# Small reciprocal roots as one GpSimd power, and a broadcast read with step zero

## The chip, the cores and the metric

The kernel runs on one core of one Trainium2 chip. Its time is the device time of one execution in microseconds (us); lower is better. The engines named below are TensorE (PE, with its weight loads shown as PEld), VectorE (DVE), ScalarE (ACT), GpSimd (POOL) and SyncE (SP), which work side by side and wait for one another through semaphores.

## The reference

The program is a small two-layer encoder over 512 positions of width 1024, all in 32-bit floats. Layer 0 mixes with an RWKV-7 recurrence (12 heads of 64) beside a 4-head attention into 256 memory tokens; layer 1 uses chunked attention beside the same kind of memory attention. Each layer ends with a convolutional gated feed-forward block. What matters here are its reciprocal roots:

```
def rms_norm(x, g):
    xf = x.astype(jnp.float32)
    y = xf * lax.rsqrt(jnp.mean(xf * xf, axis=-1, keepdims=True) + RMS_EPS)
    return (y * g.astype(jnp.float32)).astype(x.dtype)
...
kk = kk / jnp.maximum(jnp.sqrt(jnp.sum(kk * kk, axis=-1, keepdims=True)), 1e-12)
...
y = (y - mean) * lax.rsqrt(var + LN_X_EPS) * per_head(lnx_w) + per_head(lnx_b)
```

The first is a norm over the width of each position, and there are seven uses of it in the kernel (the input, the memory, one before each feed-forward block, one between the layers, and the last one in two halves). The other two are per head and position: the length of the key, and the variance of the recurrence's output.

## The kernel before, in words

Activations lie transposed: 128 features on the partitions, the 512 positions along the free axis, eight such tiles for the width. A weight tile of 128 x 1024 is loaded (`load_w`), split into a rounded part and a remainder (`split_w`, L169 to L175), and `dense` multiplies with three matmuls per 128 x 128 block: L198 and L199 with the rounded weight, L203 with its remainder. While `lo_on` is set, in the middle of layer 0, the remainder isn't made by a DVE subtraction (L175) but by an ACT pass (L172) and an accumulating DMA that the GpSimd queue issues (L173).

Layer 0's mixer goes over six pairs of heads. `prepare(i)` projects key, receptance and value of a pair, normalises the key, and solves a triangular system per chunk with a long row of small DVE instructions (L662 to L669: `X`, tile Xs, with the product in Xu). `front(i)` builds the matrices of the pair's eight chunks, and `back(i)` runs the recurrence over them and normalises its output. `weave` interleaves three such generators: back of pair i-1, front of pair i, prepare of pair i+1. A generator yields a cost and a wait in ns; `weave` gives the turn to the one that is furthest behind its share, and a yielded wait holds that generator back by so much on weave's own clock. The stream that results isn't the final order: a planner of the language places each instruction on its engine by priority (the order of the stream) and by when it reckons the operands ready, with its own durations for each instruction. So an instruction that it takes to be late lets later ones pass, on each engine apart.

The roots are used in two helpers.

`head_rsqrt` (L541) is used once in `prepare` through `keys` (L626, the key's length) and once in `back` (L850, the output's variance), so twelve times in all. The squares of a 128 x 512 tile are summed by four small matmuls per call into eight columns (L550), a DVE instruction adds or clamps (`fix`, tile hra), `rsqrt_small` makes the roots, the generator yields 700 with a wait of 3000, a DVE copy spreads each column over 64 columns (L556), and four PE transposes (L559) turn the result so that it can be multiplied with the tile.

`norm_rho` (L242) is used seven times. Four matmuls against a column of 1/1024 (L245, two in the last norm's halves and in the memory's), a DVE addition of the epsilon (L247, tile rha), `rsqrt_small` on four or two columns, a DVE copy that spreads each column over 128 (L252), PE transposes (L255) and an ACT copy into `rho` (L256), which scales the projections as they leave PSUM.

`rsqrt_small` (L219) works on 128 x n values with n of 8, 4 or 2: one DVE instruction makes a first guess from the bits of the number (L222), and three Newton rounds of three DVE instructions each (L224, L225, L226) follow, so ten dependent instructions on DVE.

Of the kernel before, what the change touches and what calls it, by code (L numbers as in the profile page):

```python
# [111 lines left out]
def trunk_kernel(ctx, tc, A, out):  # L112
# [17 lines left out]
    acc = cp.tile([P, S], F32, name="acc")  # L130
    rho = cp.tile([P, S], F32, name="rho")
    rc = cp.tile([P, 4], F32, name="rc")

    def C(name, lo=0, n=None):
        o, w = COFF[name]
        return cst[:, o + lo:o + lo + (w if n is None else n)]
# [23 lines left out]
    def tmp(dt=F32, shape=(P, S)):  # L160
        return banks["tmp"].tile(list(shape), dt, name="tmp", tag="tmp")
# [54 lines left out]
        V.tensor_tensor(l_, src, h_, op=ALU.subtract)  # L216


    def rsqrt_small(pool, a, n):  # L219
        r = pool.tile([P, 8], F32, name="rsq", tag="rsq")  # L220
        q = pool.tile([P, 8], F32, name="rsq2", tag="rsq2")
        V.tensor_scalar(r[:, :n].bitcast(I32), a.bitcast(I32), -0.5, 1597463007.0, op0=ALU.mult, op1=ALU.add)  # L222
        for _ in range(3):
            V.tensor_tensor(q[:, :n], r[:, :n], r[:, :n], op=ALU.mult)  # L224
            V.scalar_tensor_tensor(q[:, :n], q[:, :n], -0.5, a, op0=ALU.mult, op1=ALU.mult)  # L225
            V.scalar_tensor_tensor(r[:, :n], q[:, :n], 1.5, r[:, :n], op0=ALU.add, op1=ALU.mult)  # L226
        return r


    def norm_tile(src, m, gain, h_, l_):  # L230
        sq = acc if m == 0 else tmp()
# [10 lines left out]
    def norm_rho(acc_, rho_, n=4, rc_=None):  # L242
        ps = ps_s()
        for t in range(n):
            PE.matmul(ps[:, 2 * t:2 * t + 2], acc_[:, t * P:(t + 1) * P], C("ones_d"), start=True, stop=True)  # L245
        a = cp.tile([P, 8], F32, name="rha", tag="rha")
        V.tensor_scalar(a[:, :n], ps[:, 0:2 * n:2], RMS_EPS, None, op0=ALU.add)  # L247
        r = rsqrt_small(cp, a[:, :n], n)
        if rc_ is not None:
            V.tensor_copy(rc_[:, :n], r[:, :n])  # L250
        bc = tmp()
        V.tensor_copy(bc[:, :n * P].rearrange("p (t c) -> p t c", c=P), r[:, :n].unsqueeze(2).to_broadcast([P, n, P]))  # L252
        pt = ps_s()
        for t in range(n):
            PE.transpose(pt[:, t * P:(t + 1) * P], bc[:, t * P:(t + 1) * P], C("ident"))  # L255
        SC.copy(rho_, pt[:, :n * P])  # L256

    def mem_attention(l, score, cost, dst, pr_tile, pt_tile):
# [139 lines left out]
    def kt_(name, shape=(P, S), bufs=None, dt=F32):  # L398
        if bufs is None:
            return kp.tile(list(shape), dt, name=name, tag=name)  # L400
        return kp.tile(list(shape), dt, name=name, tag=name, bufs=bufs)
# [141 lines left out]

    I64 = COFF["i64"][0]

    def head_rsqrt(sq, sel, fix, bank):

        ps = bank()
        for t in range(4):
            PE.matmul(ps[:, 2 * t:2 * t + 2], sq[:, t * P:(t + 1) * P], C(sel), start=True, stop=True)  # L550
        a = kt_("hra", (P, 8), bufs=2)
        fix(a[:], ps[:, 0:8])
        r = rsqrt_small(kp, a[:], 8)
        yield 700, 3000
        bc = tmp()
        V.tensor_copy(bc[:].rearrange("p (g c) -> p g c", c=64), r[:].unsqueeze(2).to_broadcast([P, 8, 64]))  # L556
        pt = bank()
        for t in range(4):
            PE.transpose(pt[:, t * P:(t + 1) * P], bc[:, t * P:(t + 1) * P], C("ident"))  # L559
        yield pt  # L560
# [5 lines left out]
    def prepare(i, T):  # L566
# [54 lines left out]
        def keys():  # L621
# [1 line left out]
            SC.activation(kn[:], k[:], AF.Copy, scale=kneg[:, i:i + 1])  # L623
            sq = tmp()
            SC.activation(sq[:], kn[:], AF.Square)
            hr = head_rsqrt(sq, "hs1", lambda o, p: V.tensor_scalar(o, p, 1e-24, None, op0=ALU.max), ps_s)  # L626
            yield next(hr)
            pr_ = next(hr)
            V.tensor_tensor(kn[:], kn[:], pr_[:], op=ALU.mult)
# [138 lines left out]
    def back(i, T, dst, tiles=own_tiles, go=None):  # L768
# [78 lines left out]
        sq = tmp()  # L847
        SC.activation(sq[:], yc[:], AF.Square)
        yield 0, 1700
        hr = head_rsqrt(sq, "hsm", lambda o, p: V.tensor_scalar(o, p, LN_X_EPS, None, op0=ALU.add), ps_s)  # L850
        yield next(hr)
        pr_ = next(hr)
        if go is not None:
# [427 lines left out]
```

## Time and profile before

| what | value |
|---|---|
| median of three runs | 1376.41 us (1375.87 to 1377.62) |
| profiled execution, span from the first to the last instruction | 1375.2 us |
| PE busy | 1320.1 us, 96% of the span |
| DVE busy | 827.1 us, 60% |
| ACT busy | 612.6 us, 45% |
| POOL busy | 34.0 us, 2%, in 55 instructions |
| mean granted TensorE clock | 0.989 |

The profile is of an execution of its own, so its span stands beside the median of the timed runs, 1.2 us below it; a time of that execution other than its span isn't on the page. A busy share is an average over stages: from about 55 us to 390 us layer 0's mixer runs, with many small instructions on PE and DVE; the two feed-forward blocks (about 410 to 775 us and 1000 to 1365 us) are rows of large matmuls; layer 1's attention lies between them. In the rows, a line such as `L224 DVE TENSOR_TENSOR rsq<-rsq` is an instruction of line 224 on DVE that writes and reads the tile rsq; in the chain of waits each row has its start, its length and the instruction that the end of the program goes back to.

### The profile page before, as it was taken

How to read it: one execution, taken by the hardware profiler on the slowest of the kernel's cores; microseconds unless marked ns; L12 is line 12 of the kernel's file. 1: busy time of each engine (PE TensorE's matmuls, PEld its weight loads, DVE VectorE, ACT ScalarE, POOL GpSimd, SP SyncE). 2: the span in 40 equal slices, each digit the busy share in tenths (PEclk: the TensorE clock that was granted, in tenths of full speed). 3: DMA queues.
4: the chain of work that ended last, by engine and by line, in shares of the span. 5: the costliest groups of instructions: out<-in, count | busy, mean ns of one | idle time of the engine just before them, and what ended most of it. 6: DMA issues, size and time to landing. Idle time of an engine off the chain costs nothing.

```text
span 1375.2 us, 20877 instructions
## 1 busy us (share of the span) xinstructions
PE 1320.1 (96%) x8266; PEld 1073.8 (78%) x8266; DVE 827.1 (60%) x1752; ACT 612.6 (45%) x1022; POOL 34.0 (2%) x55
## 2 busy tenths in 40 slices
PE   6989999999799999999999999999999999999996
PEld 4877777777588888888888878786788888888886
DVE  7876788878356655655333667657665565563324
ACT  6556565555234333333222566657443333332321
POOL 3000000000000000000000000000000000000000
PEclk9999999999899999999999999999999999999998
DMA  5366544462132233233232422222223223223332
GB/s 181 112 181 135 107 104 111 104 135 50 52 117 92 92 100 100 92 97 99 84 98 85 157 87 85 82 94 94 92 92 107 92 93 103 96 88 86 106 91 75
DMA packets 63507, 139.18 MB, mean 101 GB/s; under 512 B 24625, under 2 KB 28337, under 8 KB 63409
## 3 DMA queue, kind: packets, MB, share of 16 engines
q1 hardware_dynamic: 60672, 127.89, 29.8%
q0 software_dynamic: 2736, 9.96, 4.2%
q8 instruction: 65, 1.06, 0.3%
q14 instruction: 34, 0.27, 0.1%
HBM read 131.01 MB, written 6.82 MB: 100 GB/s over the span
## 4 chain that ended last, share of the span: by engine, by line
PE 78%; DVE 12%; ACT 4%; DMA 3%; issue 2%; SPq 0%; DVEq 0%; ACTq 0%; POOLq 0%
PE psf L198 12%; PE psf L199 12%; PE psf L203 12%; PE psd L198 10%; PE psd L199 10%; PE psd L203 10%; DVE Xu L667 2%; DVE Xs L669 1%; PE pss L1098 1%; DVE Xs L662 1%; DVE ML L720 1%; DVE wlo L175 1%; PE psd L1048 1%; PE pss L297 1%; ACT whi L169 1%
## 5 line engine op out<-in xcount | busy, mean ns | idle before, releaser
L175 DVE TENSOR_TENSOR wlo<-wraw,whi 128x1024 fp32r<-128x1024 f32 x183 | 219.0, 1197 | 132.3 <-PE psd L203 118.2
L169 ACT CAST whi<-wraw 128x1024 fp32r<-128x1024 f32 (+1 forms) x202 | 207.8, 1030 | 163.9 <-DMA wraw<-in_ffn_out_dram 41.5
L198 PE MATMUL psd<-r1h,whi 128*128 128x512 f32 x336 | 137.6, 410 | 7.5 <-ACT r1h L215 3.8
L198 PE MATMUL psf<-r2h,whi 128*128 128x512 f32 x352 | 137.1, 390 | 0.0
L198 PE MATMUL psf<-r1h,whi 128*128 128x512 f32 x352 | 137.1, 390 | 0.0
L199 PE MATMUL psf<-r1l,whi 128*128 128x512 f32 x352 | 136.9, 389 | 0.0
L199 PE MATMUL psf<-r2l,whi 128*128 128x512 f32 x352 | 136.9, 389 | 0.0
L199 PE MATMUL psd<-r1l,whi 128*128 128x512 f32 x336 | 134.9, 401 | 0.2 <-DVE r1l L216 0.2
L203 PE MATMUL psd<-r1h,wlo 128*128 128x512 f32 x336 | 91.3, 403 | 3.9 <-DMA wlo<-in_wA_dram 3.9
L199 PE MATMUL psd<-f3l,whi 128*128 128x512 f32 (+1 forms) x238 | 88.6, 377 | 0.0
L198 PE MATMUL psd<-f3h,whi 128*128 128x512 f32 (+1 forms) x238 | 88.5, 376 | 0.0
L359 DVE TENSOR_TENSOR tmp<-psf,rho 128x512 f32<-128x512 f32 x44 | 30.4, 692 | 94.7 <-PE psf L203 94.7
L203 PE MATMUL psf<-r1h,wlo 128*128 128x512 f32 x352 | 86.9, 389 | 0.0
L203 PE MATMUL psf<-r2h,wlo 128*128 128x512 f32 x352 | 86.9, 389 | 0.0
L198 PEld LDWEIGHTS psd<-r1h,whi 128*128 128x128 f32 x336 | 65.0, 193 | 23.7 <-ACT r1h L215 4.0
L198 PE MATMUL psd<-r2h,whi 128*128 128x512 f32 (+1 forms) x200 | 77.0, 389 | 0.8 <-ACT r2h L1105 0.7
L199 PE MATMUL psd<-r2l,whi 128*128 128x512 f32 (+1 forms) x200 | 76.4, 385 | 0.7 <-DVE r2l L216 0.7
L198 PEld LDWEIGHTS psf<-r2h,whi 128*128 128x128 f32 x352 | 66.1, 188 | 13.7
L199 PEld LDWEIGHTS psf<-r1l,whi 128*128 128x128 f32 x352 | 66.1, 188 | 13.7
L203 PEld LDWEIGHTS psf<-r1h,wlo 128*128 128x128 f32 x352 | 66.1, 188 | 13.7
L203 PEld LDWEIGHTS psf<-r2h,wlo 128*128 128x128 f32 x352 | 66.1, 188 | 13.7
L199 PEld LDWEIGHTS psf<-r2l,whi 128*128 128x128 f32 x352 | 66.1, 188 | 13.6
(352 smaller groups left out, 2420.9 us busy)
## 6 DMA issues: line engine op xcount, KB each, us to landing
wraw<-in_ffn_in_dram SPq DMA_DIRECT2D x88, 512.0 KB, 3.3
wraw<-in_ffn_out_dram SPq DMA_DIRECT2D x32, 448.0 KB, 3.3
wraw<-in_wA_dram SPq DMA_DIRECT2D x20, 512.0 KB, 3.9
wlo<-in_wA_dram POOLq DMA_DIRECT2D x17, 512.0 KB, 8.0
wraw<-in_w_out_dram SPq DMA_DIRECT2D x16, 512.0 KB, 3.4
wraw<-in_ffn_out_dram SPq DMA_DIRECT2D x16, 512.0 KB, 4.2
wraw<-in_wB_dram SPq DMA_DIRECT2D x8, 512.0 KB, 3.4
Lr<-d SPq DMA_DIRECT2D x24, 128.0 KB, 6.3
```

The costliest lines, as they stand in the source:

```text
L169: SC.copy(hi[:, :n], raw)
L175: V.tensor_tensor(lo[:, :n], raw, hi[:, :n], op=ALU.subtract)
L198: PE.matmul(ps, wh[:, j * P:(j + 1) * P], ah, start=start and n == 0, stop=False)
L199: PE.matmul(ps, wh[:, j * P:(j + 1) * P], al, start=False, stop=False)
L203: PE.matmul(ps, wl[:, j * P:(j + 1) * P], act(k)[0], start=False, stop=stop and n == len(ks) - 1)
L297: PE.matmul(pso[hs, :], vm[l][:, kt, (f * 2 + hh) * 64:(f * 2 + hh + 1) * 64], pts[f, hh, kt], start=kt == 0, stop=kt == 1)
L359: V.tensor_tensor(v[:], pv[:], rho[:], op=ALU.mult)
L662: V.scalar_tensor_tensor(X[:, m, q + 1:], L1[:, :, 0], X[:, m, q:q + 1], X[:, m, q + 1:], op0=ALU.mult, op1=ALU.add)
L667: V.tensor_tensor(uv, L1.rearrange("p i o -> p o i").to_broadcast([P, k, n]), X[:, 0:k, q:q + 1].to_broadcast([P, k, n]), op=ALU.mult)
L669: V.tensor_tensor(X[:, 0:k, q + 1:], X[:, 0:k, q + 1:], uv, op=ALU.add)
L720: V.tensor_tensor(ML[:, h, c4 * 4:c4 * 4 + 4, 0:128], ps[h][:], C("m1").unsqueeze(1).to_broadcast([P, 4, 128]), op=ALU.mult)
L1048: PE.matmul(pt, r1h[:, k, ts], wh[:, ws], start=k == 0, stop=False)
```

## The change

`rsqrt_small` now takes the sums in PSUM themselves, with the operation (addition or maximum) and the epsilon. One DVE instruction writes the sum with its epsilon to a tile `rsa`, and one GpSimd `tensor_tensor` with the operation `pow` raises it to the power -0.5, which is read from a tile `mhalf` that a memset fills at the start. The caller's own addition (`fix` in `head_rsqrt`, L247 in `norm_rho`) is that one DVE instruction now. The yield in `head_rsqrt` has a wait of 2000 in place of 3000. In `norm_rho` the DVE copy that spread the columns (L252) is gone; the PE transposes read the column of roots itself with step zero. In `head_rsqrt` the copy (L556) stays.

```diff
+    mhalf = cp.tile([P, 8], F32, name="mhalf")
+    GP.memset(mhalf[:], -0.5)
...
-    def rsqrt_small(pool, a, n):
+    def rsqrt_small(pool, src, n, op, eps):
         r = pool.tile([P, 8], F32, name="rsq", tag="rsq")
-        q = pool.tile([P, 8], F32, name="rsq2", tag="rsq2")
-        V.tensor_scalar(r[:, :n].bitcast(I32), a.bitcast(I32), -0.5, 1597463007.0, op0=ALU.mult, op1=ALU.add)
-        for _ in range(3):
-            V.tensor_tensor(q[:, :n], r[:, :n], r[:, :n], op=ALU.mult)
-            V.scalar_tensor_tensor(q[:, :n], q[:, :n], -0.5, a, op0=ALU.mult, op1=ALU.mult)
-            V.scalar_tensor_tensor(r[:, :n], q[:, :n], 1.5, r[:, :n], op0=ALU.add, op1=ALU.mult)
+        a = pool.tile([P, 8], F32, name="rsa", tag="rsa")
+        V.tensor_scalar(a[:, :n], src, eps, None, op0=op)
+        GP.tensor_tensor(r[:, :n], a[:, :n], mhalf[:, :n], op=ALU.pow)
         return r
...
-        a = cp.tile([P, 8], F32, name="rha", tag="rha")
-        V.tensor_scalar(a[:, :n], ps[:, 0:2 * n:2], RMS_EPS, None, op0=ALU.add)
-        r = rsqrt_small(cp, a[:, :n], n)
+        r = rsqrt_small(cp, ps[:, 0:2 * n:2], n, ALU.add, RMS_EPS)
         if rc_ is not None:
             V.tensor_copy(rc_[:, :n], r[:, :n])
-        bc = tmp()
-        V.tensor_copy(bc[:, :n * P].rearrange("p (t c) -> p t c", c=P), r[:, :n].unsqueeze(2).to_broadcast([P, n, P]))
         pt = ps_s()
         for t in range(n):
-            PE.transpose(pt[:, t * P:(t + 1) * P], bc[:, t * P:(t + 1) * P], C("ident"))
+            PE.transpose(pt[:, t * P:(t + 1) * P], r[:, t:t + 1].to_broadcast([P, P]), C("ident"))
         SC.copy(rho_, pt[:, :n * P])
...
-    def head_rsqrt(sq, sel, fix, bank):
+    def head_rsqrt(sq, sel, op, eps, bank):
...
-        a = kt_("hra", (P, 8), bufs=2)
-        fix(a[:], ps[:, 0:8])
-        r = rsqrt_small(kp, a[:], 8)
-        yield 700, 3000
+        r = rsqrt_small(kp, ps[:, 0:8], 8, op, eps)
+        yield 700, 2000
...
-            hr = head_rsqrt(sq, "hs1", lambda o, p: V.tensor_scalar(o, p, 1e-24, None, op0=ALU.max), ps_s)
+            hr = head_rsqrt(sq, "hs1", ALU.max, 1e-24, ps_s)
...
-        hr = head_rsqrt(sq, "hsm", lambda o, p: V.tensor_scalar(o, p, LN_X_EPS, None, op0=ALU.add), ps_s)
+        hr = head_rsqrt(sq, "hsm", ALU.add, LN_X_EPS, ps_s)
```

## The prediction, written before the result was known

> **What bounds the kernel now.** I read the head of the page, then the table by stretches, then the rows of the tile rsq, the waits, and last the chain and the timeline around the roots.
>
> ```profile
> span 1375.2 us, 20877 instructions
> PE 1320.1 (96%) x8266; PEld 1073.8 (78%) x8266; DVE 827.1 (60%) x1752; ACT 612.6 (45%) x1022; POOL 34.0 (2%) x55
> ...
> PE 78%; DVE 12%; ACT 4%; DMA 3%; issue 2%; SPq 0%; DVEq 0%; ACTq 0%; POOLq 0%
> ```
>
> PE bounds the kernel, so a DVE instruction is worth something only where PE waits for it. The table by stretches (length, busy time and count of PE, PEld, DVE, ACT, POOL, then clock and DMA) shows where that can be:
>
> ```profile
> 55.00:390.00 335.00, 311.00 (x3506) 244.59 (x3506) 247.97 (x799) 178.73 (x332) 16.54 (x19) 0.97 0.47 112
> 405.00:640.00 235.00, 235.00 (x1044) 194.46 (x1043) 138.55 (x184) 89.73 (x110) 0.00 (x0) 1.00 0.29 96
> ```
>
> In the feed-forward block PE has no gap at all. In the mixer it has 24.0 us of gaps (335.0 - 311.0), and DVE is busy for 248 us. Twelve of the nineteen roots are there. The rows of the tile rsq give the number and the duration (min/median/max, ns):
>
> ```profile
> L224 DVE TENSOR_TENSOR rsq<-rsq x57: 134/161/699, 25.2 to 1366.4; 128x8 f32<-128x8 f32 x36, 128x4 f32<-128x4 f32 x12, 128x2 f32<-128x2 f32 x9
> L222 DVE TENSOR_SCALAR rsq<-hra x12: 116/165/172, 56.0 to 363.7; 128x8 int32<-128x8 int32 x12
> L222 DVE TENSOR_SCALAR rsq<-rha x7: 163/169/170, 24.7 to 1365.0; 128x4 int32<-128x4 int32 x4, 128x2 int32<-128x2 int32 x3
> L252 DVE COPY tmp<-rsq x7: 286/419/427, 31.3 to 1367.0; 128x512 f32<-128x512 f32 x4, 128x256 f32<-128x256 f32 x3
> ```
>
> Line 224 runs three times per root, so 57 means 19 roots of ten instructions, about 0.165 us each. DVE loses 19 x 10 x 0.165 = 31 us of work, and 7 copies of about 0.4 us. That is a load, not a time. What PE waits for is in the waits (total us, times, longest), first for the mixer, then for the whole program, then for the first 55 us:
>
> ```profile
> PE pss L559 <- DVE Xu L667: 3.1, 4, 0.8
> PE pss L559 <- DVE tmp L556: 1.1, 4, 0.3
> ...
> PE pss L255 <- DVE tmp L252: 3.7, 3, 2.6
> ...
> PE psd L198 <- ACT whi L169: 1.1, 1, 1.1
> PE pss L255 <- DVE tmp L252: 0.8, 1, 0.8
> ```
>
> PE stands 0.8 us before the transposes of four key norms and 0.3 us before those of four others, and 2.6 us once at the very end.
>
> **The end of the program.** Here nothing else runs, and the chain (start, length, what) shows the root bare:
>
> ```profile
> 1365.05 0.18 DVE rsq L222
> ...
> 1366.82 0.17 DVE rsq L226
> ...
> 1367.01 0.30 DVE tmp L252
> 1367.32 0.14 issue
> 1367.45 0.67 PE pss L255 x2
> ```
>
> From the first root instruction to the transposes 2.40 us pass. In their place stand a hop to GpSimd, one power on two columns, and a hop to PE. For a hop to PE I take the 0.14 above, for the one to GpSimd 0.10, an estimate near it.
>
> The power itself is in no row. The nearest rows of its engine (line, names, shapes, count, then busy us and mean ns) and one of the timeline:
>
> ```profile
> L433 POOL MEMSET E<- 128x8 f32 x1 | 0.1, 112 | 0.0
> L173 POOL DMA_DIRECT2D wlo<-in_wA_dram x17 | 14.8, 871 | 227.2 <-ACT wlo L172 169.6 <-DVE ML L720 53.0 <-ACT wah L215 2.6
> ...
> 18.35 2.16 POOL L463 TENSOR_TENSOR Rq<-Rq,tmp 128x512 f32<-128x512 f32 x1
> ```
>
> Bounds for eight columns: not under 0.11, since an instruction of that shape that computes nothing takes it; above, 2.2, the longest POOL row. I write P for it and take 1.2 us, about halfway, and near the 0.87 of the DMA issue, the only other row in which this engine runs a routine rather than one operation per element. For two columns I take P/3 = 0.4. The end gains 2.40 - 0.24 - 0.4 = 1.8 us (2.05 at P = 0.11, 1.4 at 2.2).
>
> **The twelve roots of the mixer** are of two kinds. In four key norms (from 142 us on) the solve's instructions keep DVE busy. The chain there:
>
> ```profile
> 227.69 0.08 DVE rsq L222
> ...
> 230.78 0.07 DVE rsq L226
> 230.85 0.18 DVE Xs L669
> 231.03 0.34 DVE tmp L556
> 231.37 0.17 DVE Xu L667
> 231.53 0.61 PE pss L559 x4
> ```
>
> Root instructions slip between dependent solve instructions and add 0.07 to 0.08 each, ten of them 0.75 us. They go. But the root also ends late, 230.85, and PE waits its 0.8. With the power, the root is there P + 0.1 after the sum (which is there before 227.7), about 229.0, so that wait can close: 3.1 us for the four. Against this stands what the power does to DVE. The timeline (start, duration, engine) when GpSimd added tiles in the prologue:
>
> ```profile
> 34.34 0.73 POOL L473 TENSOR_TENSOR W<-W,tmp 128x256 f32<-128x256 f32 x1
> 34.97 1.23 DVE L175 TENSOR_TENSOR wlo<-wraw,whi 128x1024 fp32r<-128x1024 f32 x1 [0.57 <-ACT whi L169]
> 35.14 1.65 POOL L473 TENSOR_TENSOR W<-W,tmp 128x256 f32<-128x256 f32 x1
> ...
> 25.18 0.70 DVE L224 TENSOR_TENSOR rsq<-rsq 128x4 f32<-128x4 f32 x1
> ```
>
> Alone, the GpSimd addition takes 0.73; while DVE subtracts two tiles in SBUF it takes 1.65. A root instruction of 0.16 took 0.70 beside such an addition. They take turns, one whole instruction at a time. The solve reads two tiles in SBUF at every step, so I charge P in full: four times (0.75 - P), and the 3.1. The Trainium skill's page GPSIMD Engine Reference, section Key points, says that GpSimd shares its SBUF interfaces with VectorE and contends with its two-input instructions; those rows agree (1.65 against 0.73). Did the lock cover only the power's reads, the four would cost next to nothing: a gain of 6.1 instead of 1.3.
>
> The other eight (two early key norms and six of the recurrence's output) are bare delays:
>
> ```profile
> 249.53 0.12 DVE L222 TENSOR_SCALAR rsq<-hra 128x8 int32<-128x8 int32 x1
> ...
> 251.75 0.17 DVE L226 SCALAR_TENSOR_TENSOR rsq<-rsq,rsq 128x8 f32<-128x8 f32 x1
> 251.95 0.43 DVE L556 COPY tmp<-rsq 128x512 f32<-128x512 f32 x1
> ```
>
> The ten take 10 x 0.197 = 2.0 us (nine steps from 1365.05 to 1366.82 at the end give the step); instead come a hop, P and a hop back, taken as 0.15 together, so 1.85 - P each. PE's own wait there is only 0.3, as it has projections to run meanwhile; but ACT and DVE wait for the result to finish the output. Between nothing and all I take half: 4 x (1.85 - P). The DVE copy behind the power waits for it, and with it, DVE being in order, the solve and the next evictions; that wait is in P.
>
> So the mixer gains 3.1 + 4(0.75 - P) + 4(1.85 - P) = 13.5 - 8P: 3.9 us at 1.2, 12.6 at 0.11, -4.1 at 2.2.
>
> GpSimd's queue also issues the weights' DMAs in order. The power may stand behind one that still waits for ACT:
>
> ```profile
> 245.81 0.86 POOL L173 DMA_DIRECT2D wlo<-in_wA_dram  x1 [9.58 <-ACT wlo L172]
> 263.74 0.86 POOL L173 DMA_DIRECT2D wlo<-in_wA_dram  x1 [17.07 <-ACT wlo L172]
> ```
>
> The roots nearby start no earlier than 249.5 (above) and 267.3 (its matmuls, below), after these issues, so I cost it at nothing; a clash costs at most 0.86 if the issue is under way. The issues get later by at most P, against gaps of 9 us and more.
>
> **The rest.** In the prologue the first root is stretched over 24.7 to 31.3 us by the additions of GpSimd above, and ACT and PE wait for what follows. The two PE waits of the first 55 us make 1.9; I take 1.5 (0 to 1.9), as the projections of that time fill PE anyway. The other roots of whole norms run beside projections: 3.7 less 0.8 and 2.6 leaves 0.3. The seven copies that go are inside these terms; transposes that read a column with step zero I take as unchanged, bounded by doubling them (0.67 more at the end). The memset of `mhalf` is 0.11 in the first microsecond, while the first loads are under way.
>
> Sum: 3.9 + 1.5 + 0.3 + 1.8 = 7.5 us. The span of 1375.2 becomes 1367.7; the median stands 1.2 above the span, so 1376.4 - 7.5 = 1368.9.
>
> A last unknown is the order. The planner reorders around the shorter waits (2000 for 3000) and what it reckons for the power. How much order alone moves shows in how evenly pairs follow one another:
>
> ```profile
> 182.46 1.05 PE L550 MATMUL pss<-cst,tmp 128*128 128x2 f32 x8
> ...
> 225.42 0.83 PE L550 MATMUL pss<-cst,tmp 128*128 128x2 f32 x6
> ...
> 267.32 1.05 PE L550 MATMUL pss<-cst,tmp 128*128 128x2 f32 x8
> ```
>
> Three key norms follow one another after 42.96 and 41.90 us, so like pairs differ by 1.1. Over six pairs I allow 2.5 either way.
>
> **The rivals.**
> - *PE bounds the mixer as it is*: it is 93% busy there, and what the roots free is filled or held by something else. Then only 1.5 + 0.3 + 1.8 = 3.6 remain: 1372.8. For it: 311 of 335 us; against: the 4.2 us of waits at L559.
> - *DVE's relief is worth more*: of 24 us of gaps many end on late DVE work, and the power is short. At P = 0.11 the sum is 12.6 + 1.9 + 0.3 + 2.05 = 16.9: 1359.5. By the skill's GPSIMD Engine Reference, section Engine selection, a two-input instruction is about twice as slow as on VectorE; two times the 0.165 above is 0.33, an estimate, and the sum would be 15 us. No row shows a power.
> - *A long power stops DVE* (the slower side): the power runs in software, holds the port for all its length, and the DVE copy behind it stops DVE in order. All terms together are 13.5 - 8P + 1.8 + 2.16 - P/3, which is zero at P = 2.1 us; from there the change loses. At 5 us it is 24 lost: 1400. For it: the exclusive turns above; against: no POOL row is over 2.2.
> - *The first power is slow*: if it takes as long as the stretched root it replaces (6.6 us, 24.7 to 31.3), the prologue's 1.5 is lost: 1370.4. The same reference, section Instruction dispatch, gives some 6 us for the first call of freshly loaded code. No run here shows it.
>
> **How the numbers follow.** My sum 0.47, own range 1363 to 1374; PE bound 0.17; larger relief 0.13; first power slow 0.07; long power 0.16. The range must hold the bounds of P (1359.5 to 1376.4 + 4.1 - 1.0 - 0.3 - 1.4 = 1377.8) and the order: 1358 to 1380; the long power is left out. A measurement of this kernel tells about 0.2% (2.8 us) from no change, so faster means under 1373.7: 0.45 of my sum's 0.47, half of the PE rival, all of the larger relief, 0.06 of the slow first one, 0.72; same 0.12; slower 0.16.
>
> **What would show it.** One POOL power row per root with its mean (P right if 0.8 to 1.6); no rsq rows on DVE; DVE busy about 30 us lower, less what lock waits add; the waits before L559 under 1.5 us in sum; the end from sum to transposes at about 0.8 us instead of 2.4. Solve rows (L667, L669) with maxima near 1 us would show the turns. A power over 2.1 us, or powers behind DMA issues, would make it wrong.

## The result and the profile after

The changed kernel is slower: 1401.41 us median (1400.27 to 1404.37, four runs) against 1377.01 (1375.87 to 1378.16, four runs) of the kernel before; ratio 1.0176, 95% interval 1.0157 to 1.0195. The forecast was 1368.9, with a range of 1358 to 1380.

The head of the page and the shares of the chain of waits, of the kernel after:

```profile
span 1398.5 us, 20712 instructions
PE 1336.6 (96%) x8266; PEld 1080.7 (77%) x8266; DVE 802.5 (57%) x1555; ACT 613.8 (44%) x1022; POOL 61.0 (4%) x75
...
PE 76%; DVE 10%; issue 6%; ACT 4%; POOL 2%; DMA 1%; DVEq 0%; POOLq 0%; SPq 0%; ACTq 0%
PE psf L205 11%; PE psf L201 11%; PE psf L200 11%; PE psd L200 9%; PE psd L201 9%; PE psd L205 9%; POOL rsq L225 2%; DVE Xu L659 2%; DVE Xs L661 1%; PE pss L1090 1%; PE pss L291 1%; PE psd L1040 1%; DVE Xs L654 1%; PE pss L1076 1%; PE pss L281 1%
```

POOL has 2% of the chain that ended last, all of it the power (`POOL rsq L225`). DVE does 24.6 us less work (827.1 to 802.5), as planned, and the span is 23.3 us longer (1375.2 to 1398.5).

The power, by shape (count, then busy us and mean ns), and the waits that name it (total us, times, longest), of the kernel after:

```profile
L225 POOL TENSOR_TENSOR rsq<-rsa,mhalf 128x8 f32<-128x8 f32 x12 | 20.4, 1697 | 121.4 <-DVE rsa L224 121.4
L225 POOL TENSOR_TENSOR rsq<-rsa,mhalf 128x4 f32<-128x4 f32 x4 | 4.5, 1122 | 110.8 <-DVE rsa L224 110.8
L225 POOL TENSOR_TENSOR rsq<-rsa,mhalf 128x2 f32<-128x2 f32 x3 | 3.0, 1006 | 372.4 <-DVE rsa L224 372.4
```

```profile
DVE tmp L548 <- POOL rsq L225: 18.5, 12, 1.9
...
PE pss L551 <- DVE tmp L548: 6.7, 6, 1.5
PE pss L636 <- DVE Xs L661: 6.2, 3, 2.3
...
PE pss L636 <- DVE Xu L659: 1.7, 1, 1.7
```

P, the prediction's name for the power's length, is 1.70 us for eight columns. At each of the twelve head roots DVE stands at the spreading copy (L548, formerly L556): 18.5 us in all. PE stands at the transposes (L551, formerly L559) for 6.7 us where it stood 4.2, and for 7.9 us at L636, which waits for the solve (6.2 for one of the solve's tiles and 1.7 for the other; at that line, formerly L644, it stood 1.3 before, for another tile). One such root, from the timeline of the kernel after (start, length, engine):

```profile
191.51 0.17 DVE L224 TENSOR_SCALAR rsa<-pss 128x8 f32<-128x8 f32 x1
191.63 0.28 DVE L659 TENSOR_TENSOR Xu<-Lr,Xs 128x75 f32<-128x75 f32 x1
193.53 0.43 DVE L548 COPY tmp<-rsq 128x512 f32<-128x512 f32 x1 [1.62 <-POOL rsq L225]
193.87 0.23 DVE L661 TENSOR_TENSOR Xs<-Xs,Xu 128x75 f32<-128x75 f32 x1
```

```profile
191.83 1.66 POOL L225 TENSOR_TENSOR rsq<-rsa,mhalf 128x8 f32<-128x8 f32 x1 [13.79 <-DVE rsa L224]
```

The copy is the second instruction behind the sum in DVE's order. The solve's next step (L661) has its operands at 191.9 and starts at 193.87, only because it is behind the copy. In the order of the kernel before, eleven instructions of the solve stand between the sum and the copy at this root and at the three key norms like it, among the root's own (its rows are in the experiment pow_old_order, below).

At the roots of the recurrence's output DVE had next to nothing else to do between the sum and the copy before either. There PE is left with less: between the sum's matmuls and the transposes stood 13 to 17 matmuls at the four such roots from 160 to 310 us, and 4 or 5 stand there now. The transposes of one of them, before and after:

```profile
252.43 0.66 PE L559 MATMUL pss<-cst,tmp 128*128 128x128 f32 x4 [0.29 <-DVE tmp L556]
```

```profile
264.61 0.66 PE L551 MATMUL pss<-cst,tmp 128*128 128x128 f32 x4 [1.27 <-DVE tmp L548]
```

At these four roots PE stood 0.9 us in all and stands 5.3 now, most of the 6.7 above. At the four key norms from 140 us on its waits before the transposes did close, from 3.1 us to 0.2.

The planner put the copy right behind the sum. With an addition in the power's place it makes the same order, instruction for instruction on PE, DVE and ACT (short_op, below), so it reckons the power like any short operation.

Where the 23.7 us were lost is read from four markers: the matmuls that sum the squares of the first, the third and the sixth key norm, and the first matmul of the feed-forward block. From the timelines the third and the sixth key norm, in the kernel before and then after:

```profile
140.67 1.05 PE L550 MATMUL pss<-cst,tmp 128*128 128x2 f32 x8
...
267.32 1.05 PE L550 MATMUL pss<-cst,tmp 128*128 128x2 f32 x8
```

```profile
144.69 1.05 PE L544 MATMUL pss<-cst,tmp 128*128 128x2 f32 x8
...
282.41 1.05 PE L544 MATMUL pss<-cst,tmp 128*128 128x2 f32 x8
```

The rows of the first feed-forward matmul (min/median/max ns, then first and last start), before and after:

```profile
L198 PE MATMUL psf<-r2h,whi x352: 387/389/481, 412.2 to 650.9; 128*128 128x512 f32 x176
```

```profile
L200 PE MATMUL psf<-r2h,whi x352: 389/389/478, 435.9 to 675.0; 128*128 128x512 f32 x176
```

The first key norm's marker goes from 53.95 to 58.20: 4.2 us are lost by then. Up to the third key norm nothing more is lost (86.7 and 86.5 us). The three pairs take 137.7 instead of 126.7 (45.9 and 42.2 us a pair): 11.1. From there to the block 153.5 instead of 144.9: 8.6. After the block nothing is lost, and the end gains. The last root, from the timeline of the kernel after:

```profile
1390.01 0.16 DVE L224 TENSOR_SCALAR rsa<-pss 128x2 f32<-128x2 f32 x1 [0.83 <-PE pss L243]
1390.25 0.70 POOL L225 TENSOR_TENSOR rsq<-rsa,mhalf 128x2 f32<-128x2 f32 x1 [8.91 <-DVE rsa L224]
1391.00 0.43 PE L249 MATMUL pss<-cst,rsq 128*128 128x128 f32 x2 [1.10 <-POOL rsq L225]
```

From the end of the sum (1390.17) to the transposes pass 0.83 us; before it was 2.43, from 1365.02 (the sum started at 1364.86 and took 0.16) to 1367.45.

### The profile page after: what moved, and what is told of

Read it like the earlier page. It is cut to its first block, busy times and chain, and to the rows that moved or that the text cites. A ratio compares the mean times of both kernels' runs of the same rounds, so it can differ in the third digit from the quotient of the medians.

```text
span 1398.5 us, 20712 instructions
## 1 busy us (share of the span) xinstructions
PE 1336.6 (96%) x8266; PEld 1080.7 (77%) x8266; DVE 802.5 (57%) x1555; ACT 613.8 (44%) x1022; POOL 61.0 (4%) x75
## 3 DMA queue, kind: packets, MB, share of 16 engines
q8 instruction: 65, 1.06, 0.3%
## 4 chain that ended last, share of the span: by engine, by line
PE 76%; DVE 10%; issue 6%; ACT 4%; POOL 2%; DMA 1%; DVEq 0%; POOLq 0%; SPq 0%; ACTq 0%
PE psf L205 11%; PE psf L201 11%; PE psf L200 11%; PE psd L200 9%; PE psd L201 9%; PE psd L205 9%; POOL rsq L225 2%; DVE Xu L659 2%; DVE Xs L661 1%; PE pss L1090 1%; PE pss L291 1%; PE psd L1040 1%; DVE Xs L654 1%; PE pss L1076 1%; PE pss L281 1%
## 5 line engine op out<-in xcount | busy, mean ns | idle before, releaser
L200 PEld LDWEIGHTS psf<-r1h,whi 128*128 128x128 f32 x352 | 66.1, 188 | 13.7
```

The lines of the kernel that those rows point to most:

```text
L200: PE.matmul(ps, wh[:, j * P:(j + 1) * P], ah, start=start and n == 0, stop=False)
```

## The experiments

Fifteen kernels ran. What is compared is, for each: B, the start of the first feed-forward matmul in its profile (412.2 before, 435.9 after); the time of a pair, a third of the time from the third to the sixth key norm (42.2 and 45.9); M, the mean duration of the large matmuls (psf from r1h and whi) in the second feed-forward block; and the ratio to the kernel before. The six kernels whose instructions stand in the order of the kernel before up to the last norm (that kernel, dummy, pow_old_order, before_pad, last_pow, last_pow_fit) have B from 409.5 to 414.3, so B is known to some 2.5 us either way. From B to the end of the profile the kernels with an M of 389 take 960 to 963 us and the others 968 to 972 (the reason is under "The second feed-forward block"). So the totals of the others hold some 8 us that no root caused, and their medians, all but before_pad's, lie above the times that were expected.

| kernel | B, us | pair, us | M, ns | ratio, 95% interval |
|---|---|---|---|---|
| after | 435.9 | 45.9 | 389 | 1.0176 (1.0157 to 1.0195) |
| short_op | 416.2 | 42.2 | 394 | 1.0061 (1.0038 to 1.0085) |
| short_op_fit | 418.3 | 42.2 | 389 | 0.9999 (0.9979 to 1.0018) |
| norm_pow | 418.3 | 42.2 | 389 | 1.0024 (1.0004 to 1.0044) |
| head_pow | 435.0 | 47.0 | 395 | 1.0224 (1.0200 to 1.0247) |
| head_short | 418.8 | 42.2 | 396 | 1.0091 (1.0074 to 1.0108) |
| dummy | 411.4 | 42.3 | 396 | 1.0082 (1.0051 to 1.0114) |
| head_act | 425.4 | 43.9 | 389 | 1.0137 (1.0105 to 1.0168) |
| head_pool | 435.8 | 46.2 | 389 | 1.0156 (1.0138 to 1.0174) |
| wait6000 | 448.6 | 49.9 | 389 | 1.0227 (1.0192 to 1.0261) |
| newton_normstep | 413.6 | 42.2 | 395 | 1.0077 (1.0053 to 1.0101) |
| pow16 | 457.9 | 50.6 | 393 | 1.0379 (1.0360 to 1.0398) |
| last_pow | 414.3 | 42.3 | 393 | 1.0060 (1.0039 to 1.0082) |
| pow_old_order | 411.6 | 42.3 | 389 | 1.0016 (0.9996 to 1.0037) |
| before_pad | 412.9 | 42.2 | 396 | 1.0062 (1.0038 to 1.0086) |
| last_pow_fit | 409.5 | 42.2 | 389 | 1.0001 (0.9984 to 1.0019) |

**The length of the power.** `short_op` keeps the order of the changed kernel and makes the power short (it leaves out the roots):

```diff
...
-        V.tensor_scalar(a[:, :n], src, eps, None, op0=op)
-        GP.tensor_tensor(r[:, :n], a[:, :n], mhalf[:, :n], op=ALU.pow)
+        V.tensor_scalar(a[:, :n], src, 0.0, None, op0=ALU.mult)
+        GP.tensor_tensor(r[:, :n], a[:, :n], mhalf[:, o:o + n], op=ALU.add)
...
```

> Every power of the changed kernel becomes a GpSimd addition of the same shape, 0.1 to 0.3 us where the power takes 1.0 to 1.7; the order of instructions on every engine stays that of the changed kernel (two more fills at the start). Left out are the roots: VectorE writes the sum times zero and GpSimd adds a constant near a typical root, so the data stay in range. Theory W (the power's length counts, because the spreading copy stands right behind it in VectorE's order, 12 x 1.5 us of standing and what follows from it): most of the 24 us comes back, 1370 to 1384. Rival O (the new order of work alone is worse, with any operation in the power's place): stays at 1390 or more. Rival C (less TensorE clock in the changed kernel's mixer, 0.95 against 0.97, for a reason outside the waits): stays at 1390 or more too, and the mixer's clock stays at 0.95.

B falls to 416.2 and the pairs are back at 42.2 us: of the 23.7 us lost at the block, 19.7 go with the length alone. The time of 1385.69 is above theory W's range all the same; why, M says (below). `pow16` makes the power of the heads longer in the same order:

```diff
...
-        GP.tensor_tensor(r[:, :n], a[:, :n], mhalf[:, :n], op=ALU.pow)
+        w = 2 if n == 8 else 1
+        GP.tensor_tensor(r[:, :w, :n], a[:, :n].unsqueeze(1).to_broadcast([P, w, n]), mhalf[:, :w, :n], op=ALU.pow)
...
```

> The changed kernel, with each of the twelve head powers computing its eight columns twice (128x16, the second eight read by nobody); order of work as in the changed kernel. From 1.01 us for 4 columns and 1.70 for 8 the power should take about 3.0. Theory U (the length that the planner doesn't count is paid at each root by engines that stand in order): the step from short_op (0.3 us, feed-forward block at 416.0) to the changed kernel (1.70 us, 435.7) is 19.7 us for 12 x 1.40, 1.17 per us; 12 x 1.3 us more make 18, the block starts at 450 to 458 and the time is 1414 to 1424. Rival V (a threshold that is passed already, or a cost per power and not per microsecond): the block under 442, the time under 1408.

```profile
L226 POOL TENSOR_TENSOR rsq<-rsa,mhalf 128x16 f32<-128x16 f32 x12 | 35.5, 2960 | 121.8 <-DVE rsa L224 121.8
```

B is 457.9, in the range of theory U; the time, 1431.01, is 7 above it, with an M of 393. From 0.23 us (short_op_fit) over 1.70 to 2.96 for each of the twelve roots, B goes from 417.3 (mean of the two short ones) over 435.9 to 457.9: 1.06 us of time for each us of power, and then 1.45. One profile stands behind each of these, and other kernels give other sizes: head_pow less head_short 0.92 by B, the changed kernel less short_op_fit 1.28 by their medians. So the length is paid about whole; that a longer one costs more than its length rests on pow16 alone.

**Which roots.** `norm_pow` has powers and step zero in the seven whole norms alone, `head_pow` in the twelve head roots alone (the others are ten DVE operations, as before). `head_short` is `head_pow` with an addition for each power (it leaves out the twelve roots). Their edits against the changed kernel, in this order (`rsqrt_newton` is the old root with its addition in front):

```diff
-        r = rsqrt_small(kp, ps[:, 0:8], 8, op, eps)
-        yield 700, 2000
+        r = rsqrt_newton(kp, ps[:, 0:8], 8, op, eps)
+        yield 700, 3000
```

```diff
-        r = rsqrt_small(cp, ps[:, 0:2 * n:2], n, ALU.add, RMS_EPS)
+        r = rsqrt_newton(cp, ps[:, 0:2 * n:2], n, ALU.add, RMS_EPS)
...
+        bc = tmp()
+        V.tensor_copy(bc[:, :n * P].rearrange("p (t c) -> p t c", c=P), r[:, :n].unsqueeze(2).to_broadcast([P, n, P]))
...
-            PE.transpose(pt[:, t * P:(t + 1) * P], r[:, t:t + 1].to_broadcast([P, P]), C("ident"))
+            PE.transpose(pt[:, t * P:(t + 1) * P], bc[:, t * P:(t + 1) * P], C("ident"))
```

```diff
...
+        V.tensor_scalar(a[:], src, 0.0, None, op0=ALU.mult)
+        GP.tensor_tensor(r[:], a[:], mhalf[:], op=ALU.add)
...
-        r = rsqrt_small(kp, ps[:, 0:8], 8, op, eps)
+        r = head_short(kp, ps[:, 0:8])
```

> Powers and the step-zero reading in the seven whole norms alone; the twelve roots per head stay ten VectorE operations. Theory W: the twelve heads carry all of the loss but the first 4 us, so 1375 to 1380: the end gains its 1.7, and the prologue's norms (first key root at 59.75 against 56.0) may lose up to 4. If the prologue's shift of 4 us comes from the powers of the norms, the first key root is at 59 to 60 here and the time at 1379; if it is made by the heads' order, the first key root stays at 56 and the time falls to 1374 or 1375. Rival L (any power on GpSimd slows VectorE and with it the rest by contention, wherever it stands): 7 of 19 powers, 1384 or more.

> Powers in the twelve roots per head alone; the seven whole norms keep ten VectorE operations and their spreading copy. Theory W: nearly all of the loss, 1396 to 1404 (24.4 plus the 1.7 that the end no longer gains, less the prologue's 4 if the norms make that). Rival L: 12 of 19 powers, near 1392. If the whole norms made the loss: 1380 or less.

> The order of work of the run with powers in the heads alone (head_pow: block at 434.7, pairs 47 us apart), with a GpSimd addition in the place of each of its twelve powers; the whole norms are those of before, with ten VectorE operations. The roots of the heads are left out (sum times zero plus a constant). Theory U: the pairs return to the 42.0 us of the kernel before and no less, the block starts at 411 to 417 against 412.0 before, the time 1374 to 1382: even a root that costs 0.3 us gains nothing in the mixer. Rival D (VectorE's relief is worth the 4 to 12 us that the forecast counted): the block at 400 to 408, the time 1364 to 1372. Rival O (the order alone costs): 420 or later.

The heads carry it: B 435.0 with their powers, 418.8 with short operations in the same order (just above theory U's 411 to 417 and under rival O's 420). The pairs tell more: 42.2 us with a root that costs 0.23 us, and 42.2 before, with ten DVE operations. So the DVE work that was taken away (two roots a pair, nine instructions of some 0.165 us each, 3 us) was worth nothing to the pairs in this order. Rival D's gain didn't come, and with it the relief that the forecast counted. That the relief was there and the new order took as much back isn't excluded: no run takes this work away in the old order. In the windows (length, then PE, PEld, DVE, ACT, POOL busy, clock, DMA) of the kernel before, after and short_op_fit:

```profile
140.00:290.00 150.00, 143.52 (x1873) 111.16 (x1870) 123.20 (x441) 86.54 (x157) 9.49 (x11) 1.00 0.49 104
```

```profile
140.00:290.00 150.00, 139.68 (x1771) 107.03 (x1770) 111.19 (x352) 78.87 (x143) 20.66 (x17) 0.98 0.45 98
```

```profile
140.00:290.00 150.00, 146.29 (x1888) 112.19 (x1887) 120.22 (x379) 86.82 (x156) 10.73 (x18) 1.00 0.49 107
```

In the same 150 us PE gets through 1873 instructions before, 1771 after, and 1888 with the short operation.

`norm_pow` takes 1381.36 us, just above theory W's 1375 to 1380 and under rival L's 1384. It loses its 6.1 us before the block too, 4.1 of them before its first key norm (at 58.00). In the prologue the power stands in GpSimd's queue behind additions and a memset; the timeline of the kernel after, and the window from 25 to 30 us, before and then after:

```profile
23.45 2.74 POOL L467 TENSOR_TENSOR W<-W,tmp 128x256 f32<-128x256 f32 x3
23.94 0.16 DVE L224 TENSOR_SCALAR rsa<-pss 128x4 f32<-128x4 f32 x1 [0.28 <-PE pss L243]
26.14 0.52 POOL L461 MEMSET acc<- 128x512 f32 x1
26.62 1.03 POOL L225 TENSOR_TENSOR rsq<-rsa,mhalf 128x4 f32<-128x4 f32 x1
27.71 1.12 PE L249 MATMUL pss<-cst,rsq 128*128 128x128 f32 x4 [2.55 <-POOL rsq L225]
```

```profile
25.00:30.00 5.00, 5.00 (x18) 3.98 (x17) 5.00 (x10) 0.00 (x0) 3.65 (x4) 0.76 0.00 0
```

```profile
25.00:30.00 5.00, 2.45 (x9) 2.01 (x9) 1.59 (x3) 1.17 (x4) 4.05 (x7) 0.50 0.00 0
```

The root is done at 27.65 instead of 31.3, and the time is lost all the same: PE, which in the old order had projections to run beside the root, is put behind the transposes and stands 2.55 us; from 25 to 30 us the granted clock is 0.50 instead of 0.76. `newton_normstep` has no power at all (`rsqrt_newton` in both places, as in the first two diffs of this group), only the step-zero reading of the whole norms:

> No power at all: ten VectorE operations for each root as before, and only the whole norms' transposes read the column with step zero. It separates what shifts the first key root from 56.0 to 59.7 us. If it is the power of the first norm, which stands behind additions in GpSimd's queue (its sum is there at 23.94, it starts at 26.62): the first key root is back at 55 to 57 and the time 1374 to 1377 (the end gains the copy's 0.3 to 0.45). If it is the new order of the prologue that comes with the copy's removal: 59 to 60, and 1378 to 1381.

The expectation goes by the first root of a key, which starts 1.5 to 2 us behind the marker used here: at 56.00 before, at 59.75 in the changed kernel, and at 58.37 in this one. That lies in neither of its two ranges, so each cause has a share. The markers say the same: the first key norm is from 52.99 to 55.63 in kernels in the old order, at 56.33 here, at 56.92 and 57.01 in short_op and short_op_fit, and from 58.00 to 58.93 in those with a power there. By the means of the three groups, 54.4, 56.8 and 58.4, some 2.4 of the 4.0 us come with the new order alone and the rest with the power.

**Does the power disturb by being there?** `dummy` runs a power beside each head root of the kernel before, for nobody:

```diff
...
+        du = kp.tile([P, 8], F32, name="dum", tag="dum")
+        GP.tensor_tensor(du[:], a[:], mhalf[:], op=ALU.pow)
         r = rsqrt_small(kp, a[:], 8)
```

> The kernel before, with one power of 128x8 on GpSimd beside each of the twelve roots per head, on the same sum, whose result nobody reads; the roots stay ten VectorE operations, nothing waits for a power. It prices what the powers take from VectorE by their mere presence (shared reading, GpSimd's queue of transfers). Theory W: nothing, 1375 to 1379. Rival L (the power holds what it shares with VectorE for its length, 12 x 1.66 = 20 us of it): 1385 to 1397, and VectorE rows of 1 us and more beside the powers.

The time of 1387.45 is rival L's. The profile isn't: B is 411.4, the mixer lost nothing, and all of the 8 us is in the second feed-forward block, where no power runs. Reading the total alone, I would have taken the wrong theory.

**Who stands.** `head_act` and `head_pool` move the copy behind the head powers to ScalarE and to GpSimd (the latter with `GP.tensor_copy`):

```diff
-        V.tensor_copy(bc[:].rearrange("p (g c) -> p g c", c=64), r[:].unsqueeze(2).to_broadcast([P, 8, 64]))
+        SC.copy(bc[:].rearrange("p (g c) -> p g c", c=64), r[:].unsqueeze(2).to_broadcast([P, 8, 64]))
```

> The changed kernel, with the spreading copy behind the twelve head powers on ScalarE instead of VectorE, so nothing on VectorE waits for a power. Theory W (VectorE standing at the copy, 12 x 1.6 us, is the loss of the mixer; short_op put it at 19.7 us at the start of the feed-forward block): most of it comes back, the feed-forward block's first matmul at 416 to 424 us against 435.7, the time 1380 to 1390, and ScalarE shows the waits for rsq in VectorE's place. Rival T (TensorE standing at the transposes is the loss, whichever engine copies): 1395 or more.

> The changed kernel, with that copy on GpSimd, right behind the power on the same engine: no engine but TensorE waits for the root. The GpSimd copy of 128x512 isn't in any trace so far; the nearest rows are its fill of that shape (0.53 us) and its addition (1.2 to 2.2 us). Theory W: VectorE is free of the waits, the first feed-forward matmul at 414 to 425 us, the time 1378 to 1391. Rival T: TensorE waits 2 to 3 us at each root, 1395 or more.

No DVE instruction waits for a head power any more in them. With ScalarE half of the pairs' loss is gone (43.9 us, B 425.4, in the fastest of its executions), but the median is 1397.21, beyond the range of theory W; with GpSimd, whose copy takes 0.69 us, nothing comes back. The waits of head_pool, and then the same row of the kernel after:

```profile
DVE tmp L849 <- PE pss L551: 16.1, 6, 3.4
...
PE pss L551 <- POOL tmp L548: 7.8, 5, 1.9
```

```profile
DVE tmp L849 <- PE pss L551: 4.8, 6, 1.5
```

DVE stands one step later, at the product with the spread root (L849), 16.1 us instead of 4.8. PE stands too: at the four roots of the recurrence's output from 160 to 310 us it waits 1.5 us each before the transposes in head_act, with five matmuls in front. So theory W, with its copy, was too narrow: whatever comes next in an engine's order and needs the root makes that engine stand. The planner moved much other work in both kernels as well, so what the copy alone is worth isn't told apart. `wait6000` announces a longer wait in the generator:

```diff
-        yield 700, 2000
+        yield 700, 6000
```

> The changed kernel, with the wait that its generator announces behind the power 6000 instead of 2000. The copy still stands right behind the sum in VectorE's order in all twelve roots (one to three instructions between). Theory W: no relief, 1394 to 1406, and VectorE's waits for rsq stay at 16 to 19 us. If the shorter announced wait were the cause (work placed too early everywhere): 1385 or less.

No relief: a pair takes 49.9 us, the ratio is 1.0227. The generator's wait orders the stream; the planner still puts the copy right behind the sum, with none or one instruction between in eleven of the twelve roots. It moved other work too, and why a pair takes 4 us longer than in the changed kernel isn't settled.

**The length or the order?** `pow_old_order` keeps the order of the kernel before and puts the same power on the path:

```diff
+        GP.tensor_tensor(du[:, :n], a, mhalf[:, :n], op=ALU.pow)
...
-            V.scalar_tensor_tensor(r[:, :n], q[:, :n], 1.5, r[:, :n], op0=ALU.add, op1=ALU.mult)
+                V.scalar_tensor_tensor(r[:, :n], q[:, :n], 0.0, du[:, :n], op0=ALU.mult, op1=ALU.add)
...
```

The whole norms keep two of their small tiles in one here, so that the tiles behind them lie where they lay before.

> The kernel before in its own order, with the root of each of the twelve heads taken from a power on GpSimd: the ten VectorE operations stay, but the last of them multiplies its work by zero and adds the power's result, so that the power of 1.70 us (with its hops) lies on the path from the sum to the copy, beside nine VectorE operations of 1.8 us in all. Theory U (the loss is the length that the order doesn't know, so engines stand in order): nothing is lost, the feed-forward block starts at 409 to 414 against 412.0 before and 435.7 in the changed kernel, the time is 1374 to 1380. Rival (the power itself, its hops or its sharing with VectorE cost): the block at 420 or later, 1385 or more.

One of its roots in the timeline, on DVE and on GpSimd:

```profile
184.53 0.16 DVE L643 TENSOR_SCALAR hra<-pss 128x8 f32<-128x8 f32 x1
184.65 0.23 DVE L686 TENSOR_TENSOR Xs<-Xs,Xu 128x70 f32<-128x70 f32 x1
184.80 0.17 DVE L224 TENSOR_SCALAR rsq<-hra 128x8 int32<-128x8 int32 x1
184.92 0.27 DVE L684 TENSOR_TENSOR Xu<-Lr,Xs 128x65 f32<-128x65 f32 x1
...
187.31 0.16 DVE L233 SCALAR_TENSOR_TENSOR rsq<-rsq,dum 128x8 f32<-128x8 f32 x1
188.10 0.42 DVE L573 COPY tmp<-rsq 128x512 f32<-128x512 f32 x1
```

```profile
184.84 1.66 POOL L226 TENSOR_TENSOR dum<-hra,mhalf 128x8 f32<-128x8 f32 x1 [6.26 <-DVE hra L643]
```

B 411.6, pairs of 42.3 us, ratio 1.0016 with an interval that holds 1. The same twelve powers of 1.70 us on the same path cost nothing that can be measured where the order of work leaves the time for them: on DVE the solve's steps run beside the power, as above, and on PE 13 to 17 matmuls stand before the transposes of the recurrence's output again, where it waits 0.36 us at most. The cause is both together: a length that the order doesn't know.

**The second feed-forward block.** M is 389 ns in one half of the kernels and 393 to 396 in the other; the half with 389 is, by the sources, just the one in which the small tiles of the norms take as many bytes as before. `before_pad` adds one unused tile of 32 bytes per partition to the kernel before; `short_op_fit` and `last_pow_fit` repeat two kernels with the tiles at their old addresses (short_op_fit reads its constants with step zero; last_pow_fit keeps two small tiles in one).

```diff
     rc = cp.tile([P, 4], F32, name="rc")
+    pad = cp.tile([P, 8], F32, name="pad")
+    GP.memset(pad[:], 0.0)
```

> The kernel before, with one unused tile of 32 bytes per partition and its fill at the start; every instruction and its order stays, the weights' tiles (and what is allocated behind them) lie 32 bytes further, while the tile r1h that the second feed-forward block multiplies with them stays. If the address makes the slower pace: matmuls of that block at 395 or 396 ns instead of 389, the time 1383 to 1387. If it is chance of the single run: 389 ns and 1375 to 1379.

> short_op once more (additions in the powers' place, roots left out, the changed kernel's order), with all tiles at the addresses of the changed kernel; the constants are one column read with step zero. If the address made its second block slow: matmuls at 389 ns there and a time of 1377 to 1381, which is the changed kernel less 20 to 24 us. If not: 1384 to 1388 again.

The rows of before_pad and of the kernel before, from 1030 to 1230 us:

```profile
L200 PE MATMUL psf<-r1h,whi 128*128 128x512 f32 x287 | 113.7, 396 | 0.0
```

```profile
L198 PE MATMUL psf<-r1h,whi 128*128 128x512 f32 x294 | 114.4, 389 | 0.0
```

An unused tile costs 0.6%. short_op_fit comes back to 389 ns and 1378.84 us, ratio 0.9999: the changed kernel's order with a root of 0.23 us is as fast as the kernel before, and not faster. The changed kernel has 389 ns too (its small tiles take as many bytes as before), so its own 23 us hold nothing of this.

**A version that keeps what gained.** `last_pow` takes the power and step zero in the last norm alone (`norm_rho_pow` is `norm_rho` of the changed kernel):

```diff
-                norm_rho(acc[:, ht], rho[:, ht], 2)
+                norm_rho_pow(acc[:, ht], rho[:, ht], 2)
```

> The kernel before, with the power and the step-zero reading in the last norm's two halves alone; nothing else moves. In the changed kernel the end from the sum to the transposes shrank by about 1.7 us, so 1373.5 to 1376 where the kernel before has 1376.4 on its chip, a ratio of 0.998 to 1.000: better than both kernels, if it can be told at all.

> last_pow once more (power and step-zero reading in the last norm's two halves alone, the rest in the order of before), with all tiles at the addresses of the kernel before: 1373.5 to 1376, a ratio of 0.998 to 1.000, as the end gains 1.6 us and nothing else moves; second feed-forward block at 389 ns.

With the tiles moved it is slower (1.0060), with the tiles kept its ratio is 1.0001 (0.9984 to 1.0019): the 1.6 us of the end, 0.1%, can't be told from nothing. No kernel here beats the one before.

## Why the prediction was wrong

- **The size of P** was inside its bounds and near no edge: 1.70 against 1.2, 0.70 bare for two columns against 0.4. By the forecast's own formula the mixer's gain becomes 13.5 - 13.6 = -0.1, the end 1.5, and the time 1376.4 + 0.1 - 1.5 - 0.3 - 1.5 = 1373.2. This step explains 4 of the 32 us of the miss. (In the range's upper bound the prologue stands with 1.0, where its own lowest value was 0; the range of 1358 to 1380 covers both.)
- **The step that failed** is the sentence "The DVE copy behind the power waits for it, and with it, DVE being in order, the solve and the next evictions; that wait is in P." It isn't in P. P stood in the sum against ten instructions that went, as if DVE could do other work in P as it did between them. It can only if the order puts other work there, and this order is the one that an addition gets too: DVE stood 18.5 us at the twelve copies. The same holds for PE. "PE's own wait there is only 0.3, as it has projections to run meanwhile" was read in the old order; in the new one 4 or 5 matmuls are left there, and PE stands 1.3 to 1.5 us. So the loss per us of power is 1.06 to 1.45 for each of twelve roots, where the formula had 8 P for twelve, 0.67.
- **The constant 13.5** (DVE's freed work and PE's 4.2 us of waits) failed too: with a root of 0.23 us the pairs take what they took before, and the block starts 4 to 6 us later, not 13 earlier (13.5 - 8 x 0.23 + 1.5 of the prologue). The 3.1 us of waits at the key norms closed, as said, and no pair is shorter for it. The rival "PE bounds the mixer as it is" comes nearest here: in short_op_fit PE is busy for 123.7 of the 126.5 us of the three pairs.
- **The planner's order**, allowed at 2.5 either way, costs 4.0 to 6.6 in the three kernels with short operations (B 416.2, 418.3 and 418.8), by the same markers some 3 at most by the first key norm and the rest behind the sixth. What in it is slower isn't settled.
- **The prologue** was to gain 1.5 and lost 4.2: the forecast took GpSimd's queue as clear of the powers, with its weights' DMAs in mind, and didn't look at its additions.
- **The slower rival** had half of the mechanism: the DVE copy behind the power does stop DVE in order. Its other half fell, and its zero point with it (P = 2.1; the kernel loses at 1.70). The power doesn't hold the port, so the P that the sum charged to the four key norms for turns with the solve's steps didn't come either. The changed kernel can't show it, as not one step of the solve lies inside a power there. In pow_old_order twenty of them do, the longest of 278 ns, and the rows have the maxima that they had before; here the kernel before and then pow_old_order.

```profile
L669 DVE TENSOR_TENSOR Xs<-Xs,Xu x138: 165/220/239, 85.8 to 320.9; 128x60 f32<-128x60 f32 x18, 128x66 f32<-128x66 f32 x12, 128x69 f32<-128x69 f32 x6, 128x63 f32<-128x63 f32 x6
```

```profile
L686 DVE TENSOR_TENSOR Xs<-Xs,Xu x138: 167/221/240, 84.0 to 320.2; 128x60 f32<-128x60 f32 x18, 128x66 f32<-128x66 f32 x12, 128x69 f32<-128x69 f32 x6, 128x63 f32<-128x63 f32 x6
```

- **What was right:** the end (2.43 us less 0.83, 1.6 against 1.8 forecast), the hops (0.08 from the sum to the power, 0.05 back; 0.24 was taken for both), DVE's relief (24.6 us against 31 of removed work), that the first power isn't slow (1.03 us at 26.62, under the mean of its shape, 1.12), and nothing gained or lost in the feed-forward blocks. The forecast named the mark that would show it wrong, the waits before the transposes: 1.5 at most was said, 6.7 was found. The lines of the profile before that should have warned stood in the prediction: at 227.69 to 231.53 the root's instructions and the solve's alternate, so the root's 2 us were no empty time on DVE.

## What to carry to other kernels

Moving a chain of small operations from a busy in-order engine to one long operation elsewhere is worth its relief only if somebody waited for that work, and can cost the whole length of the new operation, as here, if the order of the engine was made without knowing it. Before such a move, look what stands behind the first reader in its engine's order, and ask what the planner reckons for the new operation. Look at the other engines in the same way: here PE's order had lost the work that hid the root. Compare by markers inside the program, not by the total alone, when kernels differ in the memory that they take.

## What the runs showed that was not expected

- **A power on GpSimd costs by the column.** 1.70 us for 8 columns and 2.96 for 16 make 0.16 us a column, and 0.44 besides; an addition of the same 8 columns took 0.23. The Trainium skill's GPSIMD Engine Reference, section Engine selection, by which the forecast reckoned 0.33 for such an operation, is near for the addition (DVE's root instruction took 0.165) and not for the power.
- **The power waited for DVE, and DVE not for the power.** Two columns took 0.70 us alone and 1.62 beside a DVE subtraction of two tiles of 1.22 us, which itself wasn't lengthened (its mean is 1.197). An addition of two columns in the same place took 1.11 us in short_op_fit and 0.19 alone, so the delay is the same 0.9 us. The small steps of the solve weren't lengthened inside a power (above). From the timeline of the kernel after:

```profile
40.97 1.22 DVE L177 TENSOR_TENSOR wlo<-wraw,whi 128x1024 fp32r<-128x1024 f32 x1
...
41.13 1.62 POOL L225 TENSOR_TENSOR rsq<-rsa,mhalf 128x2 f32<-128x2 f32 x1 [11.97 <-DVE rsa L224]
```

- **The place of a tile costs 0.6%.** By the order in which the sources allocate the tiles (no view shows an address), in the second feed-forward block the operand r1h keeps its address and the weights lie 32 or 64 bytes further; the matmuls then take 393 to 398 ns instead of 389, at a granted clock of 1.00 in both. In the first block, where operand and weights move together, they stay at 389. Why that is so no run here shows.
- **PE's standing came with a lower clock.** From 20.6 to 24.0 us PE was busy for 0.99 us before and 1.15 after, and in the next 3.4 us the granted clock was 0.50 in both. There it was busy for 3.40 before and 1.16 after, and the 3.4 us behind that ran at 1.00 and at 0.50. The Trainium skill's TensorE: Matmul & The Clock Gate, section Part 1: The HAM clock gate, has the array at half its clock behind an idle window. The half agrees with these rows, though PE still worked for a third of the stretch before it. It matters in the mixer too. From the third to the sixth key norm PE has the same 1577 matmuls to run; the windows of short_op_fit, the changed kernel and pow16:

```profile
142.95:269.41 126.46, 123.71 (x1577) 95.03 (x1575) 101.04 (x315) 73.99 (x134) 9.03 (x15) 1.00 0.48 107
```

```profile
144.69:282.41 137.72, 127.40 (x1577) 96.83 (x1575) 101.37 (x315) 73.88 (x134) 18.13 (x15) 0.98 0.45 99
```

```profile
147.87:299.76 151.89, 134.59 (x1577) 101.67 (x1576) 101.76 (x316) 73.94 (x134) 25.71 (x15) 0.92 0.41 89
```

PE stands 2.8, 10.3 and 17.3 us in them, 0.9 us more for each us that the six powers in the stretch got longer. The rest of the loss is that the same matmuls take longer, 123.7, 127.4 and 134.6 us, as the clock falls from 1.00 to 0.98 and 0.92. So pow16's 1.45 us per us is standing and clock together; no run holds the clock and changes the standing.
